# A hybrid decoder step: the samples' attention in pairs and column groups, spread over the third group's attention blocks, and page copies beside the projections

## Chip, cores, metric

One core of a Trainium2 chip. The metric is device microseconds of one launch, the median of several runs; a profiled execution gives the trace. Engines are TensorE (PE, with its weight loads PEld), VectorE (DVE), ScalarE (ACT), GpSimd (POOL) and SyncE (SP), which here issues all DMAs from one queue in order.

## The reference, cut

One layer over a prompt of 2048 tokens and over 8 samples of one token each, D = 1024, f32. The mixer runs two head groups side by side: gated delta rule (4 heads) and sparse attention (4 heads, 2 key heads, 128 wide), then an output projection and a SwiGLU feed-forward of width 2816. For the samples the sparse attention reads a paged cache of 1024 past keys (8 pages of 128 tokens, found through `page_table`):

```python
score = einsum('bqh,bqhs->bqs', iw, relu(einsum('bqhd,bsd->bqhs', iq, ik_all)))  # 8 index heads of 64
_, idx = top_k(score, 256)              # of 1025 keys: 1024 from pages, 1 new
ks, vs = cache_k[phys, off], cache_v[phys, off]      # the new key where idx is the last
s = einsum('bqgrd,bqkgd->bqgrk', q, ks) * 128 ** -0.5
o = einsum('bqgrk,bqkgd->bqgrd', softmax(s), vs)     # 2 key heads g, 2 queries r each
```

The kernel does not gather: it scores all 1025 keys and gives those that aren't selected a large negative bias (L1132 adds it by a product).

## The kernel before

The program is written with tiles in pools; a planner orders each engine's instructions by a simulated timeline. Of the instructions that are ready in its simulation it takes the one that stands first in the program, so later work is pulled ahead wherever inputs and buffers allow. The tags of a pool name sets of buffers in rotation. PSUM has eight banks: "d" x4 (dense products), "g" x2 and "s" x2 (everything else).

Phase 1 (`phase1`): `project(g)` for four groups of 512 tokens, with the samples in group 0; `modulate` for the conditioning; `chunks(g)` for the delta rule; and `first_attn` for attention blocks 0 to 3 (128 tokens each). Phase 2 (`groups`): attention blocks 4 to 15 (`attn`, which calls `index` for scores and selection and `attend` for keys, softmax and values) beside feed-forward blocks `ffn(0)` to `ffn(3)`. `ffn(g)` needs attention of its own four blocks; `ffn(3)` also holds the samples' rows and needs `oTs`, the samples' mixer output. Dense products are three-fold splits (`mm3`, L157 to L159); weights come through `weights` (load at L140 or, kept, L135; split on ACT L141 and DVE L142), three tiles ahead.

In program order of `groups`: attention 4 to 7, 8 to 11, `ffn(0)`, then `copy_pages` (192 page copies, DRAM to DRAM, 64 each of index keys, keys and values, L446 and L447, each after loading the page's number into a register of SP), `sample_gdn` (the samples' delta rule), attention 12 to 15, `ffn(1)`, `sample_steps`, `ffn(2)`, `ffn(3)`.

`sample_steps` goes sample by sample. Index scores: eight transposes of [128 tokens, 64] (L1096), a copy on ACT (L1097), the heads' products with 8 columns (L1100), relu (L1101), and the weighted sum over heads with 8 columns (L1102). Selection: `select`. Keys: per sample one load of 1 MB (L1122), for each key head and half of the pages four transposes into a "g" bank (L1127), a copy on ACT (L1129) and a product with 32 columns (L1130), all accumulating in rows 0 to 31 of two "s" banks. Softmax on 32 rows. Values: one load of 1 MB per sample (L1157), eight products with 32 columns (L1164).

`attend` stores its block at L1380; `ffn` loads those at L1427, splits them at L1428 and L1429, builds rows from the modulation at L1389 and adds gated results at L1419 and L1420.

Of the kernel before, what the change touches and what calls it, by code (L numbers as in the profile page):

```python
# [34 lines left out]
NS = 8  # L35
# [20 lines left out]
WR, WI = 2, 3  # L56

# [4 lines left out]
def const_tables():  # L62
# [18 lines left out]
    s32 = np.zeros((128, 32), np.float32)  # L81
    for kv in range(2):
        for s in range(8):
            for r in range(2):
                s32[s, kv * 16 + s * 2 + r] = 1.0
    parts["s32"] = s32
    d32 = np.zeros((128, 8), np.float32)
    d32[:32] = s32[:8, :].T
    parts["d32"] = d32
    parts["pw"] = np.tile((0.5 ** np.arange(1, SEARCH + 1)).astype(np.float32), (128, 1))  # L90
    parts["io"] = np.tile(np.arange(16, dtype=np.float32), (128, 1))
    off, cols = {}, 0
    for k, v in parts.items():
        off[k] = (cols, v.shape[1])
        cols += v.shape[1]
# [9 lines left out]
CF, COFF, CL = const_tables()  # L105


class K:
# [84 lines left out]
    def build(self):  # L193
        tc, nc = self.tc, self.nc
        with ExitStack() as es:
# [10 lines left out]
            self.ikp_d = self.dr.tile([NS, 128, NPAGE, 64], F32, name="ikp_d")  # L206
# [14 lines left out]
    def consts(self):  # L221
# [4 lines left out]
        cf = self.cf = cp.tile([128, CF.shape[1]], F32, name="cf")  # L226
# [3 lines left out]
        def c(k):  # L230
            o, n = COFF[k]
            return cf[:, o:o + n]
# [7 lines left out]
        self.s32 = c("s32")  # L240
        self.d32 = c("d32")
# [13 lines left out]
        self.iqTs = cp.tile([64, NS, 8], F32, name="iqTs")  # L255
        self.ikTs = cp.tile([128, NS], F32, name="ikTs")
# [10 lines left out]
    def modulation(self):  # L267
# [34 lines left out]
        nc.sync.dma_start(self.cf[:, 128:], A["cf"][:, 128:])  # L302
# [81 lines left out]
    def phase1(self, es):  # L384
# [49 lines left out]
    def copy_pages(self):  # L434

        nc, A, tc = self.nc, self.A, self.tc
        pt_i = self.p2.tile([1, NS * NPAGE], mybir.dt.int32, name="pt_i")
        nc.sync.dma_start(pt_i, A["page_table"].rearrange("n g -> (n g)").unsqueeze(0))
        n_phys = A["cache_k"].shape[1]
        for dst, src in ((self.ikp_d, A["cache_idx_k"][0]), (self.kp_d, A["cache_k"][0].rearrange("g t h d -> g t (h d)")),  # L440
                         (self.vp_d, A["cache_v"][0].rearrange("g t h d -> g t (h d)"))):
            for s in range(NS):
                for g in range(NPAGE):
                    with tc.manual_schedule(engines={nc.sync.engine}):
                        i = s * NPAGE + g
                        pg = nc.sync.value_load(pt_i[0:1, i:i + 1], min_val=0, max_val=n_phys - 1)  # L446
                        nc.sync.dma_start(dst[s, :, g, :], src[ds(pg, 1)].rearrange("a t c -> (a t) c"))  # L447
# [78 lines left out]
    def narrow(self, g, smT, samp):  # L526
# [59 lines left out]
        for t in range(nb):  # L586
# [6 lines left out]
            if t == 4:  # L593
                nc.sync.dma_start(O[9][0, :, 0, :], ik[:NS, 0, :])
                pk = self.ps.tile([128, 512], F32, name="d", tag="d", bufs=4)
                nc.tensor.transpose(pk[:64, :NS], ik[:NS, 0, :], self.id[:NS, :NS])
                nc.scalar.copy(self.ikTs[:64], pk[:64, :NS])
                continue
# [45 lines left out]
    def tok(self, what, blk, pd, rows):  # L644
# [45 lines left out]
        else:  # L690
            self.rope(a[R].rearrange("p (h d) -> p h d", h=8), self.ri, blk, rows, 8, 8, "ropei")
            if samp:
                for h in range(8):
                    nc.tensor.transpose(pt[:64, h * rows:(h + 1) * rows], a[R, h * 64:(h + 1) * 64], self.id[R, R])
                nc.scalar.copy(self.iqTs.rearrange("p n h -> p h n"), pt[:64, :64].rearrange("p (h n) -> p h n", h=8))
# [251 lines left out]
    def sample_gdn(self):  # L947
        nc, p, A, O = self.nc, self.p2, self.A, self.O
        raws = self.raws
        tl, at = p.tile([128, 832], F32, name="gs", bufs=1), [0]  # L950
# [10 lines left out]
        def big():  # L961
            return p.tile([128, 512], F32, name="gS", tag="gS", bufs=2)
# [85 lines left out]
    def sample_steps(self, general):  # L1048
# [4 lines left out]
        def P():  # L1053
            return self.ps.tile([128, 512], F32, name="g", tag="g", bufs=2)

        def P2():
            return [self.ps.tile([128, 512], F32, name="s", tag="s", bufs=2) for _ in range(2)]

        def big():
            return q.tile([128, T], F32, name="big", tag="big", bufs=2)  # L1060

        def mid():
            return q.tile([128, 512], F32, name="PT", tag="PT", bufs=2)

        b0 = q.tile([128, T + 18], F32, name="sc", tag="sc", bufs=2)
        wk, pr = b0[:NS, 0:NK], b0[:32, NK + 16:2 * NK + 16]
        b = q.tile([128, 512], F32, name="oT", tag="oT", bufs=OB)
        PT = b[:, 0:256].rearrange("p (g r) -> p g r", g=NPAGE)
        b = b[:, 256:]
        iwT, ws, nw, dg, pnT, st = b[:8, 0:8], b[:8, 8:72], b[:8, 72:88], b[:32, 88:96], b[:NS, 96:128], b[:32, 128:131]  # L1070
        qk = b[:, 132:164]

        pw = P()
        nc.tensor.transpose(pw[:8, :8], self.iw[:NS, 16, :], self.id[:NS, :NS])
        nc.vector.tensor_copy(iwT, pw[:8, :8])
        nc.vector.memset(ws, 0.0)
        nc.vector.tensor_copy(ws[:, 0:64:9], iwT)

        pw = P()
        for s in range(NS):  # L1080
            nc.tensor.matmul(pw[:8, s:s + 1], self.iqTs[:, s, :], self.ikTs[:64, s:s + 1], start=True, stop=True)
        nc.scalar.activation(nw[:, 0:8], pw[:8, :8], AF.Relu)
        nc.vector.tensor_tensor(nw[:, 0:8], nw[:, 0:8], iwT, op=OP.mult)
        pw = P()
        nc.tensor.matmul(pw[:NS, 0:1], nw[:, 0:8], self.ones[:8, 0:1], start=True, stop=True)
        nc.vector.tensor_copy(wk[:, PAST:NK], pw[:NS, 0:1])
        psc = P2()
        for s in range(NS):
            ikp = mid().rearrange("p (g c) -> p g c", g=NPAGE)
            nc.sync.dma_start(ikp, self.ikp_d[s])  # L1090
            b = big()
            ikT, rl = b[:64, 0:1024], b[:8, 1024:2048]
            for a in range(2):
                pt = P()
                for g in range(4):
                    nc.tensor.transpose(pt[:64, g * 128:(g + 1) * 128], ikp[:, a * 4 + g, :], self.id)  # L1096
                nc.scalar.copy(ikT[:, a * 512:(a + 1) * 512], pt[:64])  # L1097
            for a, (c0, c1) in enumerate(CH):
                pd = P()
                nc.tensor.matmul(pd[:8], self.iqTs[:, s, :], ikT[:, c0:c1], start=True, stop=True)  # L1100
                nc.scalar.activation(rl[:, c0:c1], pd[:8], AF.Relu)  # L1101
                nc.tensor.matmul(psc[a][:NS], ws[:, s * NS:(s + 1) * NS], rl[:, c0:c1], start=s == 0, stop=s == NS - 1)  # L1102
        for a, (c0, c1) in enumerate(CH):
            nc.vector.tensor_copy(wk[:, c0:c1], psc[a][:NS])
# [3 lines left out]
        else:  # L1108
            self.select(q, b0[:NS], q.tile([128, T], BF, name="bias", tag="bias", bufs=2)[:NS, :NK], None, NK, NS, wk)

        qp = q.tile([128, 512], F32, name="qT", tag="qT", bufs=1).rearrange("p (k s r) -> p k s r", k=2, s=NS)
        nc.gpsimd.memset(qp, 0.0)
        for kv in range(2):
            for s in range(NS):
                c = kv * 16 + s * 2
                nc.gpsimd.tensor_copy(qp[:, kv, s, c:c + 2], self.qTs[:, kv * 2:kv * 2 + 2, s])
            nc.vector.tensor_tensor(qk[:, kv * 16:kv * 16 + 16].rearrange("p (n r) -> p r n", r=2), self.qTs[:, kv * 2:kv * 2 + 2, :],
                                    self.kTs[:, kv, :].unsqueeze(1).to_broadcast([128, 2, NS]), op=OP.mult)
        pss = P2()
        for s in range(NS):  # L1120
            kp = big().rearrange("p (g c) -> p g c", g=NPAGE)
            nc.sync.dma_start(kp, self.kp_d[s])  # L1122
            for kv in range(2):
                for a in range(2):
                    pt = P()
                    for g in range(4):
                        nc.tensor.transpose(pt[:, g * 128:(g + 1) * 128], kp[:, a * 4 + g, kv * 128:(kv + 1) * 128], self.id)  # L1127
                    kT = mid()
                    nc.scalar.copy(kT, pt)  # L1129
                    nc.tensor.matmul(pss[a][:32], qp[:, kv, s, :], kT, start=s == 0 and kv == 0, stop=False)  # L1130
        for a, (c0, c1) in enumerate(CH):
            nc.tensor.matmul(pss[a][:32], self.s32[:NS, :], wk[:, c0:c1], start=False, stop=True)  # L1132
            nc.vector.tensor_copy(pr[:, c0:c1], pss[a][:32])
        pw = P()
        nc.tensor.matmul(pw[:32, 0:1], self.s32[:NS, :], wk[:, PAST:NK], start=True, stop=False)
        nc.tensor.matmul(pw[:32, 0:1], qk, self.ones[:, 0:1], start=False, stop=True)
        nc.vector.tensor_copy(pr[:, PAST:NK], pw[:32, 0:1])
# [5 lines left out]
        pp = P()  # L1143
        for g in range(NPAGE):
# [419 lines left out]
```

## Time and profile before

| what | value |
|---|---|
| median of 3 runs | 3913.4 us (3911.79 to 3915.15) |
| the profiled execution | 3911.62 us, span 3909.8 us |
| granted TensorE clock, mean | 0.945 |
| PE busy | 3570.4 us, 91% |
| DVE, ACT, POOL busy | 55%, 39%, 17% |
| DMA | 528.56 MB, mean 135 GB/s |

The span is what the profiler saw from the first to the last instruction; the execution's own time is some 2 us longer. Busy shares are means over stages with different limits, so a change is read from the stage in which it stands: phase 1 up to about 1520 us, attention beside feed-forward up to about 3170 us, and the samples' attention and the last feed-forward block behind it.

### The profile page before, as it was taken

How to read it: one execution, taken by the hardware profiler on the slowest of the kernel's cores; microseconds unless marked ns; L12 is line 12 of the kernel's file. 1: busy time of each engine (PE TensorE's matmuls, PEld its weight loads, DVE VectorE, ACT ScalarE, POOL GpSimd, SP SyncE). 2: the span in 40 equal slices, each digit the busy share in tenths (PEclk: the TensorE clock that was granted, in tenths of full speed). 3: DMA queues.
4: the chain of work that ended last, by engine and by line, in shares of the span. 5: the costliest groups of instructions: out<-in, count | busy, mean ns of one | idle time of the engine just before them, and what ended most of it. 6: DMA issues, size and time to landing. Idle time of an engine off the chain costs nothing.

```text
span 3909.8 us, 60971 instructions
## 1 busy us (share of the span) xinstructions
PE 3570.4 (91%) x22476; PEld 2735.7 (70%) x22476; DVE 2152.3 (55%) x4423; ACT 1513.5 (39%) x2923; POOL 645.4 (17%) x577
## 2 busy tenths in 40 slices
PE   8898888898798789999988999999999999889996
PEld 4766776776586577777766887876777763567774
DVE  3555544562664565866677667676655433244444
ACT  3233223232332433554465545445553334122232
POOL 1001000000000111211131111351111222112213
PEclk9898998898899789999999999999999999999998
DMA  6663454363465334355444333344323334322221
GB/s 238 214 233 124 148 199 129 134 236 128 152 194 197 116 98 143 109 159 163 138 149 130 102 95 105 100 131 161 99 87 105 95 100 175 114 96 84 78 84 66
DMA packets 371767, 528.56 MB, mean 135 GB/s; under 512 B 46020, under 2 KB 250857, under 8 KB 369402
## 3 DMA queue, kind: packets, MB, share of 16 engines
q1 hardware_dynamic: 371458, 524.56, 41.9%
q8 instruction: 179, 2.93, 0.3%
q14 instruction: 130, 1.06, 0.1%
HBM read 427.04 MB, written 116.36 MB: 139 GB/s over the span
## 4 chain that ended last, share of the span: by engine, by line
PE 50%; DVE 8%; DMA 6%; ACT 5%; issue 4%; POOL 2%; SPq 1%; ACTq 0%; DVEq 0%; POOLq 0%
PE d L157 12%; PE d L158 12%; PE d L159 12%; PE s L1303 2%; PE g L1371 2%; DVE wi L142 2%; PE s L1346 2%; DMA wr<-in_w_ffn_in_dram 1%; ACT wi L141 1%; ACT bias L1202 1%; DMA wr<-in_w_ada_dram 1%; PE g L1365 1%; DMA wr<-in_w_ffn_out_dram 1%; PE g L173 1%; PE s L1130 1%
## 5 line engine op out<-in xcount | busy, mean ns | idle before, releaser
L142 DVE TENSOR_TENSOR wi<-wr,wi 128x512 fp32r<-128x512 f32 x712 | 527.9, 746 | 740.5 <-ACT wi L141 729.4
L141 ACT CAST wi<-wr 128x512 fp32r<-128x512 f32 x712 | 437.6, 619 | 940.9 <-PE d L159 372.2
L157 PE MATMUL d<-hh,wi 128*128 128x512 f32 x1792 | 726.7, 406 | 17.1 <-DVE th L1490 12.5
L158 PE MATMUL d<-hl,wi 128*128 128x512 f32 x1792 | 709.3, 396 | 0.0
L159 PE MATMUL d<-hh,wi 128*128 128x512 f32 x1792 | 663.8, 398 | 0.2 <-DVE wi L142 0.2
L1420 POOL TENSOR_TENSOR xt<-xt,tm 128x512 f32<-128x512 f32 x224 | 326.8, 1474 | 547.7 <-DVE tm L1419 506.2
L157 PEld LDWEIGHTS d<-hh,wi 128*128 128x128 f32 x1792 | 339.4, 189 | 104.7 <-DVE th L1490 14.8
L159 PEld LDWEIGHTS d<-hh,wi 128*128 128x128 f32 x1792 | 337.8, 189 | 83.5 <-issue 9.3
L158 PEld LDWEIGHTS d<-hl,wi 128*128 128x128 f32 x1792 | 339.5, 189 | 72.7 <-issue 7.9
L157 PE MATMUL d<-wi,hh 128*128 128x512 f32 x768 | 303.1, 415 | 16.5 <-DMA wi<-kept 10.5
L158 PE MATMUL d<-wi,hh 128*128 128x512 f32 x768 | 309.4, 403 | 0.0
L159 PE MATMUL d<-wi,hl 128*128 128x512 f32 x768 | 306.7, 401 | 0.0
L1496 POOL TENSOR_TENSOR al<-ca,ah 128x512 fp32r<-128x512 f32 x88 | 123.5, 1418 | 1062.6 <-ACT ah L1495 1002.1
L157 PE MATMUL d<-wi,ah 128*128 128x512 f32 x704 | 265.4, 410 | 17.0 <-DVE th L1490 5.6
L158 PE MATMUL d<-wi,ah 128*128 128x512 f32 x704 | 276.8, 396 | 0.5 <-DVE wi L142 0.4
L159 PE MATMUL d<-wi,al 128*128 128x512 f32 x704 | 272.2, 398 | 0.0
L1312 DVE SCALAR_TENSOR_TENSOR sc<-rl,iw,sc 128x512 f32<-128x512 f32 (+3 forms) x224 | 182.5, 815 | 81.0 <-ACT rl L1305 72.2
L1202 ACT ACTIVATE bias<-sc,sv 128x640 bf16<-128x640 f32 (+12 forms) x130 | 181.3, 1394 | 62.7 <-DVE sv L1200 39.6
L1305 ACT ACTIVATE rl<-s 128x512 f32<-128x512 f32 (+3 forms) x288 | 148.0, 543 | 113.3 <-PE s L1303 61.7
L157 PEld LDWEIGHTS d<-wi,hh 128*128 128x128 f32 x768 | 148.7, 195 | 55.9 <-DMA wi<-kept 11.2
L1419 DVE TENSOR_TENSOR tm<-d,row 128x512 f32<-128x512 f32 x224 | 150.6, 683 | 66.4 <-POOL xt L1420 32.7
L1303 PE MATMUL s<-ik,iqT 128*128 128x512 f32 (+3 forms) x576 | 161.1, 388 | 13.3 <-ACT rl L1305 10.6
(510 smaller groups left out, 5569.5 us busy)
## 6 DMA issues: line engine op xcount, KB each, us to landing
wr<-in_w_ffn_in_dram SPq DMA_DIRECT2D x704, 128.0 KB
wi<-kept SPq DMA_DIRECT2D x168, 512.0 KB
wr<-in_w_ffn_out_dram SPq DMA_DIRECT2D x176, 256.0 KB
kept<-wi SPq DMA_DIRECT2D x56, 512.0 KB
xt<-in_x_prompt_dram SPq DMA_DIRECT2D x8, 2048.0 KB
wr<-in_w_ada_dram SPq DMA_DIRECT2D x64, 256.0 KB
wr<-in_w_out_dram SPq DMA_DIRECT2D x64, 256.0 KB
wr<-in_w_in_dram SPq DMA_DIRECT2D x56, 256.0 KB
```

Of the source, the lines that this page charges most:

```text
L141: nc.scalar.copy(w[:, 0], wr)
L142: nc.vector.tensor_tensor(w[:, 1], wr, w[:, 0].bitcast(F32), op=OP.subtract)
L157: nc.tensor.matmul(out, wh, xh, start=start, stop=False, **kw)
L158: nc.tensor.matmul(out, wh, xl, start=False, stop=False, **kw)
L159: nc.tensor.matmul(out, wl, xh, start=False, stop=stop, **kw)
L1202: nc.scalar.activation(c, s, AF.Sign, bias=t, accum_out=cnt)
L1303: nc.tensor.matmul(ps[:, :w], iq[:, h, :].bitcast(F32R), B["ikT"][c * 2 + a][:, :w].bitcast(F32R), start=a == 0, stop=a == 1)
L1305: nc.scalar.activation(r[:, :w], ps[:, :w], AF.Relu)
L1312: nc.vector.scalar_tensor_tensor(s, r[:, :w], iw, s, op0=OP.mult, op1=OP.add)
L1419: nc.vector.tensor_tensor(tm[:rows], pd[:rows], rw, op=OP.mult)
L1420: nc.gpsimd.tensor_tensor(xt, xt, tm[:rows], op=OP.add)
L1496: nc.gpsimd.tensor_tensor(al[b], a, ah[b].bitcast(F32), op=OP.subtract)
```

## The change

`sample_steps` becomes a generator with four parts, and `attn` runs one part ahead of each of blocks 8 to 11:

```diff
-        self.attn(range(8, 12), B, general, 12)
+        self.attn(range(8, 12), B, general, 12, self.sample_steps(general))
         self.ffn(0)
         if not general:
-            self.copy_pages()
             self.sample_gdn()
         self.attn(range(12, 16), B, general)
         self.ffn(1)
-        self.sample_steps(general)
...
         for j, i in enumerate(blocks):
+            if part is not None:
+                next(part)
             if i not in self.biases:
```

Part 1 is the index scores and the selection, part 2 the scores of the first half of the pages, part 3 those of the second half and the softmax, part 4 the values. Index keys of two samples lie side by side in 128 rows (`ikp_d` is [4 pairs, 128, 8 pages, 2, 64]; `iqB` holds the queries of a pair as block-diagonal columns, `ikP` the new index keys), so a transpose and a product serve two samples. Products with 32 columns go to four groups of 32 PSUM rows of one bank in turn: index scores by pair, key scores by key head and sample parity, values by page modulo 4. One product over 128 rows then sums index heads, the softmax runs on 128 rows, and a product with `f4` (four stacked unit matrices) sums the four value groups:

```diff
+        for a, (c0, c1) in enumerate(CH):
+            kT = [keys(self.ikp_d[n, :, a * 4:a * 4 + 4].rearrange("p g e c -> p g (e c)")) for n in range(4)]
+            ps = P("s")
+            for n in range(4):
+                nc.tensor.matmul(ps[n * 32:n * 32 + 32], self.iqB[:, n, :], kT[n], start=True, stop=True)
+            nc.scalar.activation(rl[:, c0:c1], ps, AF.Relu)
+            pw = P()
+            nc.tensor.matmul(pw[:NS], ws, rl[:, c0:c1], start=True, stop=True)
...
+            ps = P("s")
+            nc.tensor.matmul(ps, self.s128[:NS, :], wk[:, c0:c1], start=True, stop=False, skip_group_check=True)
+            for n in range(4):
+                kT = [keys(self.kp_d[n * 2 + j % 2, :, a * 4:a * 4 + 4, j // 2 * 128:j // 2 * 128 + 128]) for j in range(4)]
+                for j in range(4):
+                    nc.tensor.matmul(ps[j * 32:j * 32 + 32], qp[:, j // 2, n * 2 + j % 2, :], kT[j], start=False, stop=n == 3, skip_group_check=True)
+            nc.scalar.copy(pr[:, c0:c1], ps)
...
+            for g2 in range(4):
+                vp = s2().rearrange("p (g c) -> p g c", g=2)
+                nc.sync.dma_start(vp, self.vp_d[s, :, g2 * 2:g2 * 2 + 2])
+                for b in range(2):
+                    g = g2 * 2 + b
+                    j = slice(g % 4 * 32, g % 4 * 32 + 32)
+                    nc.tensor.matmul(po[j, :256], z[:, g, :], vp[:, b, :], start=s == 0 and g < 4, stop=False, skip_group_check=True)
```

`keys` is new: it loads a key tile (256 KB), makes four transposes into a "g" bank and copies them on ACT. Its tiles come from a new tag "s2" of eight 2 KB buffers, longer rows from "s4" (two); `sample_gdn` draws on the same two tags, and the attention's own buffers are no longer used by the samples:

```diff
+        def keys(src):
+            kp, kT, pt = s2().rearrange("p (g c) -> p g c", g=4), s2(), P()
+            nc.sync.dma_start(kp, src)
+            for g in range(4):
+                nc.tensor.transpose(pt[:, g * 128:(g + 1) * 128], kp[:, g, :], self.id)
+            nc.scalar.copy(kT, pt)
+            return kT
```

`copy_pages(which)` moves into phase 1; the page table's tile moves from the second phase's pool to the first's:

```diff
                 self.modulate(g + 2)
                 if g == self.ng - 2:
                     self.modulate(5)
+                self.copy_pages(g)
```

`which` 0, 1 and 2 are index keys, keys and values. In `project(0)` the samples' index queries and keys are written twice, into `iqB` and `ikP`. The rotary tables (1224 columns) move to the first phase's pool and are freed after it; constants `s128`, `d128` and `f4` replace `s32` and `d32`.

More of the change, by code (lines that the diff above doesn't have):

```diff
@@ L92, in const_tables @@
     off, cols = {}, 0
+    for k in ("ra", "ri"):
+        parts[k] = parts.pop(k)
     for k, v in parts.items():
@@ L431, in phase1, with copy_pages @@
                     self.modulate(5)
+                self.copy_pages(g)
         self.ends()
-    def copy_pages(self):
+    def copy_pages(self, which):
         nc, A, tc = self.nc, self.A, self.tc
-        pt_i = self.p2.tile([1, NS * NPAGE], mybir.dt.int32, name="pt_i")
-        nc.sync.dma_start(pt_i, A["page_table"].rearrange("n g -> (n g)").unsqueeze(0))
+        if which == 0:
+            self.pt_i = self.p1.tile([1, NS * NPAGE], mybir.dt.int32, name="pt_i")
+            nc.sync.dma_start(self.pt_i, A["page_table"].rearrange("n g -> (n g)").unsqueeze(0))
+        pt_i = self.pt_i
         n_phys = A["cache_k"].shape[1]
[L440 to L447, printed above, removed]
+        dst, src = ((self.ikp_d, A["cache_idx_k"][0]), (self.kp_d, A["cache_k"][0].rearrange("g t h d -> g t (h d)")),
+                    (self.vp_d, A["cache_v"][0].rearrange("g t h d -> g t (h d)")))[which]
+        for s in range(NS):
+            for g in range(NPAGE):
+                with tc.manual_schedule(engines={nc.sync.engine}):
+                    i = s * NPAGE + g
+                    pg = nc.sync.value_load(pt_i[0:1, i:i + 1], min_val=0, max_val=n_phys - 1)
+                    to = dst[s // 2, :, g, s % 2, :] if which == 0 else dst[s, :, g, :]
+                    nc.sync.dma_start(to, src[ds(pg, 1)].rearrange("a t c -> (a t) c"))
     def load_x(self, g):
@@ L595, in narrow @@
                 pk = self.ps.tile([128, 512], F32, name="d", tag="d", bufs=4)
-                nc.tensor.transpose(pk[:64, :NS], ik[:NS, 0, :], self.id[:NS, :NS])
-                nc.scalar.copy(self.ikTs[:64], pk[:64, :NS])
+                nc.vector.tensor_copy(ik[:NS, 1, :], ik[:NS, 0, :])
+                nc.tensor.transpose(pk[:, :NS], ik[:NS].rearrange("p a c -> p (a c)"), self.id[:NS, :NS])
+                for e in range(2):
+                    nc.scalar.copy(self.ikP[e * 64:e * 64 + 64], pk[e * 64:e * 64 + 64, e:NS:2])
                 continue
@@ L692, in tok @@
             if samp:
-                for h in range(8):
-                    nc.tensor.transpose(pt[:64, h * rows:(h + 1) * rows], a[R, h * 64:(h + 1) * 64], self.id[R, R])
-                nc.scalar.copy(self.iqTs.rearrange("p n h -> p h n"), pt[:64, :64].rearrange("p (h n) -> p h n", h=8))
+                for b in range(2):
+                    x = self.m("iqs")[:NS, :512].rearrange("p (h a c) -> p h a c", h=4, a=2)
+                    for e in range(2):
+                        nc.scalar.copy(x[:, :, e, :], a[R, b * 256:(b + 1) * 256].rearrange("p (h c) -> p h c", h=4))
+                    for h in range(4):
+                        nc.tensor.transpose(pt[:, (b * 4 + h) * NS:(b * 4 + h + 1) * NS], x[:, h].rearrange("p a c -> p (a c)"), self.id[R, R])
+                for e in range(2):
+                    E = slice(e * 64, e * 64 + 64)
+                    nc.scalar.copy(self.iqB[E, :, e * 8:e * 8 + 8], pt[E, :64].rearrange("p (h n a) -> p n a h", h=8, a=2)[:, :, e, :])
                 return
@@ L1051, in sample_steps @@
         CH = ((0, 512), (512, 1024))
[L1053 to L1065, printed above, removed]
@@ L1076, in sample_steps, with P, s2 @@
-        nc.vector.memset(ws, 0.0)
-        nc.vector.tensor_copy(ws[:, 0:64:9], iwT)
-        pw = P()
[L1080 to L1083, printed above, removed]
+        def P(tag="g"):
+            return self.ps.tile([128, 512], F32, name=tag, tag=tag, bufs=2)
+        def s2():
+            return q.tile([128, 512], F32, name="s2", tag="s2", bufs=S2)
@@ L1084, in sample_steps @@
         pw = P()
-        nc.tensor.matmul(pw[:NS, 0:1], nw[:, 0:8], self.ones[:8, 0:1], start=True, stop=True)
+        nc.tensor.matmul(pw[:NS, 0:1], ws, rl[:, PAST:NK], start=True, stop=True)
         nc.vector.tensor_copy(wk[:, PAST:NK], pw[:NS, 0:1])
[L1087 to L1102, printed above, removed]
@@ L1108, in sample_steps @@
         else:
-            self.select(q, b0[:NS], q.tile([128, T], BF, name="bias", tag="bias", bufs=2)[:NS, :NK], None, NK, NS, wk)
-        qp = q.tile([128, 512], F32, name="qT", tag="qT", bufs=1).rearrange("p (k s r) -> p k s r", k=2, s=NS)
+            self.select(q, w0, s4(2 * S4, BF)[:NS, :NK], None, NK, NS, wk, "s")
+        yield
+        qp = s2()
         nc.gpsimd.memset(qp, 0.0)
+        nc.gpsimd.memset(qk, 0.0)
         for kv in range(2):
[L1114 to L1130, printed above, removed]
@@ L1153, in sample_steps @@
+        PZ = s2().rearrange("p (x g c) -> p x g c", x=2, g=NPAGE)
         nc.gpsimd.memset(PZ, 0.0)
-        po = P2()[0]
+        po = P("s")
         for s in range(NS):
-            vp, z = big().rearrange("p (g c) -> p g c", g=NPAGE), PZ[:, s % 2]
-            nc.sync.dma_start(vp, self.vp_d[s])
-            rows = lambda w, n: w[:, :, n * 2:n * 2 + 2], lambda w, n: w[:, :, 16 + n * 2:18 + n * 2]
-            for row in rows:
+            z = PZ[:, s % 2]
+            for kv in range(2):
+                c = lambda n: slice((kv * 2 + n % 2) * 8 + n // 2 * 2, (kv * 2 + n % 2) * 8 + n // 2 * 2 + 2)
@@ L1160, in sample_steps @@
                 if s >= 2:
-                    nc.gpsimd.memset(row(z, s - 2), 0.0)
-                nc.gpsimd.tensor_copy(row(z, s), row(PT, s))
-            for g in range(NPAGE):
-                nc.tensor.matmul(po[:32, :256], z[:, g, :], vp[:, g, :], start=s == 0 and g == 0, stop=False)
-        nc.tensor.matmul(po[:32, :256], pnT, self.vs[:NS, :], start=False, stop=True)
-        o = mid()[:32, :256]
-        nc.scalar.copy(o, po[:32, :256])
+                    nc.gpsimd.memset(z[:, :, c(s - 2)], 0.0)
@@ L1278, in first_attn, with attn @@
         self.attn((i0, i0 + 1), B, False)
-    def attn(self, blocks, B, general, then=None):
+    def attn(self, blocks, B, general, then=None, part=None):
         for j, i in enumerate(blocks):
+            if part is not None:
+                next(part)
             if i not in self.biases:
```

122 lines of the change are left out of this document (77 added, 45 removed).

## The prediction

> **What bounds the kernel now.** I read the page's busy times first, then busy time by stretches, then the groups of instructions, then the order of time on PE and on the DMA queue.
>
> ```profile
> span 3909.8 us, 60971 instructions
> PE 3570.4 (91%) x22476; PEld 2735.7 (70%) x22476; DVE 2152.3 (55%) x4423; ACT 1513.5 (39%) x2923; POOL 645.4 (17%) x577
> ```
> ```profile
> 0.00:400.00 400.00, 348.57 (x2439) 260.91 (x2440) 195.76 (x445) 127.84 (x286) 25.87 (x40) 0.90 0.59 201
> 1540.00:1920.00 380.00, 357.96 (x1569) 281.38 (x1569) 262.98 (x556) 194.02 (x375) 73.06 (x52) 0.99 0.50 145
> 1920.00:2130.00 210.00, 187.02 (x811) 141.55 (x811) 155.82 (x309) 120.44 (x224) 54.85 (x42) 0.96 0.43 137
> 2130.00:2600.00 470.00, 465.48 (x2131) 373.42 (x2130) 325.81 (x637) 230.57 (x377) 106.86 (x73) 1.00 0.34 103
> ```
> Columns of the second fence: stretch, length, then PE, PEld, DVE, ACT, POOL busy with counts, granted clock, DMA share, GB/s. PE bounds: from 2130 to 2600 us, where attention of one group lies beside the feed-forward block of another, it is idle for 4.5 of 470 us. An instruction added to PE there lengthens the run by its full duration; one taken out of a place where PE works alone shortens it as fully.
>
> The samples' attention is such a place. The next rows are PE's first product line of the dense layers (L157) in stretches late in the run (PE busy, PEld busy, clock, DMA).
>
> ```profile
> 3262.50:3311.60 49.10, 0.00 (x0) 0.00 (x0) 0.93 0.49 171
> 3311.60:3328.30 16.70, 0.00 (x0) 0.00 (x0) 0.88 0.34 126
> 3328.30:3368.70 40.40, 0.19 (x1) 0.26 (x2) 0.92 0.44 156
> ```
> For 106.2 us (3262.5 to 3368.7) no dense product runs: the samples' keys (49.1), softmax (16.7) and values (40.4) are alone, and the last feed-forward block waits for their result.
>
> ```profile
> L1127 PE MATMUL g<-cf,big 128*128 128x128 f32 x128 | 22.1, 300 | 0.2 <-DMA big<-kp_d 0.2
> L1130 PE MATMUL s<-PT,qT 128*32 128x512 f32 x64 | 34.7, 625 | 0.0
> L1164 PE MATMUL s<-big,iqT 128*32 128x256 f32 x128 | 31.7, 407 | 5.2 <-DMA big<-vp_d 4.2 <-POOL iqT L1162 0.9
> L1102 PE MATMUL s<-big,oT 8*8 8x512 f32 x32 | 17.4, 629 | 0.1
> L1100 PE MATMUL g<-big,iqTs 64*8 64x512 f32 x32 | 17.0, 619 | 0.0
> L1096 PE MATMUL g<-cf,PT 128*64 128x128 f32 x64 | 10.5, 289 | 0.0
> ```
> Busy us stand after the bar. Each f32 product is two instructions (L1130: 64 for 32 products), a transpose is one.
>
> **Part 1: what leaves the end of the run.** The lone 106.2 us go. The index scores (L1096, L1100, L1102) take 10.5 + 17.0 + 17.4 = 44.9 us of PE; 4.2 of them are in the lone stretch already:
>
> ```profile
> 3262.96 1.88 PE L1100 MATMUL g<-big,iqTs 64*8 64x512 f32 x4
> 3264.77 2.29 PE L1102 MATMUL s<-big,oT 8*8 8x512 f32 x4
> ```
> The other 40.7 were taken from feed-forward block 2, except for about 8 (my estimate) that filled PE's hole while block 2 hands over to block 3: that hole is late next, with no sample work to cover it. So 40.7 - 8 = 33, and 139 us leave the end.
>
> **Part 2: what is added beside the third group's attention.** Transposes: 32 for index keys (two samples share one, 64 before), 128 for keys, 8 for probabilities: 168 x 22.1/128 = 0.173, 29 us. Products 512 wide: 8 for index scores (16), 2 for the weighted sum over heads (16), 32 for keys, 2 for the mask: 44. Values: 64 products 256 wide. Their price among dense products:
>
> ```profile
> 3180.50 0.40 PE L157 MATMUL d<-hh,wi 128*128 128x512 f32 x1
> 3180.73 0.40 PE L158 MATMUL d<-hl,wi 128*128 128x512 f32 x1
> 3181.06 1.02 PE L1100 MATMUL g<-big,iqTs 64*8 64x512 f32 x2
> 3182.01 0.50 PE L159 MATMUL d<-hh,wi 128*128 128x512 f32 x1
> 3182.35 0.40 PE L157 MATMUL d<-hh,wi 128*128 128x512 f32 x1
> 3357.07 7.25 PE L1164 MATMUL s<-big,iqT 128*32 128x256 f32 x32 [1.40 <-DMA big<-vp_d]
> ```
> From start to start one wide product holds PE 0.95 us (3181.06 to 3182.01), and the steps into it and after it are 0.33 and 0.34 where dense products follow each other by 0.23 (3180.50 to 3180.73): a visit to the narrow shape costs 0.2 more. A value product costs 7.25/16 = 0.45. One by one: 29 + 44 x 0.95 + 64 x 0.45 = 100, with some 60 visits 112 us. The change writes four products into four column groups of one bank. Whether four run together the trace shows for 32x32 tiles only:
>
> ```profile
> L747 PE MATMUL g<-Dm,E 32*32 32x32 f32 x2048 | 31.8, 200 | 9.2 <-DVE Dm L742 6.5 <-issue 2.4
> L765 PE MATMUL g<-Dm,NT 32*32 32x32 f32 x256 | 13.5, 226 | 0.2 <-issue 0.2
> ```
> L747 walks four array positions and takes 15.5 ns an instruction; L765 stays in one for eight products at a time and takes 52.7: a factor of 3.4. If all packed by four, it would be 29 + (10 + 4) x 0.95 + 16 x 0.45 + 28 visits x 0.2 = 55. I take 90, nearer the upper end: a key tile becomes ready alone, after its four transposes and a 0.586 us copy on ACT (row below), so the planner will put dense work between products of one set; only the values, two pages per load, come in pairs.
>
> The Trainium skill, "TensorEngine Tiling (Array Packing)", section Key Properties, says that changing the tiling mode drains the engine; the 0.33 and 0.34 us steps agree. Its section PSUM Bottleneck says that packing speeds the products and not the evacuation, which speaks against this change, and I weigh it as a rival. "TensorE: Matmul & The Clock Gate", section Measured speedup vs the span model, gives 2.38 for three column tiles; as an estimate that would make 71 us of products 30, and the sum 31 us lower than mine; no run here shows it yet.
>
> **Part 3: what hides or uncovers.** PE idles 210 - 187 = 23 us between 1920 and 2130; sample work may fill 0 to 16, I take 8. Loads: 72 smaller ones (256 KB) replace 24. PE works in order, so a late one now stops dense work too. Bounds: 0, and 32 value loads x 1.4 us (the wait on L1164 above) = 45; I take 5, as eight buffers run ahead where there were two. The doubled index key and extra copies in the projection touch 8 rows: between 0 and 4 us, I take 1. Constants moved between pools: no added work on a path, 0.
>
> **Part 4: page copies.**
>
> ```profile
> L447 SPq DMA_DIRECT2D ikp_d<-in_cache_idx_k_dram x64: 493/502/632, 1543.7 to 1673.3; - x64
> L447 SPq DMA_DIRECT2D vp_d<-in_cache_v_dram x64: 493/500/539, 1802.2 to 1919.3; - x64
> 1546.89 3.06 SPq L447 DMA_DIRECT2D ikp_d<-in_cache_idx_k_dram  x3
> L966 SPq DMA_DIRECT2D out_dram<-in_state_conv_dram x1: 823/823/823, 35.7 to 35.7; - x1
> ACT wi L141 <- DMA wr<-in_w_ffn_in_dram: 60.1, 28, 6.0
> ACT wi L141 <- DMA wr<-in_w_ffn_in_dram: 27.8, 18, 5.2
> ```
> The last two rows are waits in 1540 to 1920 and in 2130 to 2600. The 192 copies hold SP (3.06 us for three, about 1.28 from start to start) from 1543 to 1919 with weight loads queued behind them; PE idles 22 us there against 3.6 (4.5 x 380/470) in as long a stretch without copies. So leaving gains 0 to 18. Where they go, PE idles 51.4 of the first 400 us and DMA is at 0.59. L966, also a copy from DRAM to DRAM, stands far down the program and is issued at 35.7 us: a copy that needs nothing is pulled ahead. The page copies then need only the page table and can land in the first projection. Bounds there: a loss of 0 to 36 (twice 18, as the share starts at 0.59 rather than 0.34). I take -8 and +8, net 0.
>
> **Part 5: the attention's own pace.** Sample tiles take PSUM slots "s" and "g", two each, from the blocks beside them, and a score bank is held through 16 key tiles.
>
> ```profile
> 2474.95 0.43 SPq L1380 DMA_DIRECT2D oT_d<-oT  x1
> L1015 PE MATMUL g<-gs,gS x64: 165/250/353, 2522.3 to 2603.7; 128*128 128x1 f32 x64
> 2597.81 1.56 SPq L1427 DMA_DIRECT2D ca<-oT_d  x2
> 3167.48 0.38 SPq L1380 DMA_DIRECT2D oT_d<-oT  x1
> 3171.35 0.17 PE L1074 MATMUL g<-cf,iw 8*8 8x8 f32 x1
> 3213.46 1.74 SPq L1427 DMA_DIRECT2D ca<-oT_d  x2
> 3234.35 0.40 PE L159 MATMUL d<-wi,al 128*128 128x512 f32 x1
> 3365.89 0.24 PE L1170 MATMUL g<-cf,PT 32*128 32x32 f32 x1 [0.28 <-DVE oTs L1171]
> L1129 ACT COPY PT<-g x32: 558/586/587, 3268.5 to 3318.0; 128x512 f32<-128x512 f32 x32
> ```
> L1380 stores blocks 11 and 15; L1427 are the first loads of feed-forward blocks 2 and 3: slack of 123 and 46 us. L1074 and L1170 begin and end the sample's stage, the L159 row is block 2's last dense product, L1015 the sample's delta-rule part. A key tile took 49.5/31 = 1.6 us alone; 40 tiles are 64 us, softmax about 8 (half of the 16.7 us stretch), values (no "g") half of 40: a delay D of 92. Block 2's dense work ends at 3235 in the trace, tail included about 3236; less 33, plus 90 - 8 + 5, it ends at 3290, and block 15 must be stored some 20 us earlier: D matters above 3290 - 20 - 3167 = 103. Bounds: 0, and 97 if D is the some 200 us that the sample's stage lasts (3171 to 3366, and its first loads). D is close to 103, so I take 10.
>
> **Sum**: -139 + 90 - 8 + 5 + 1 + 0 + 10 = -41. The profiled execution took 3911.6 us (span 3909.8), within 0.05% of the median 3913.4. Forecast: 3870.
>
> **Rivals.** (a) The groups pack by four and the holes fill: -139 + 55 - 16 + 2 + 1 = -97, 3815. For: L747. Against: tiles ready one by one. (b) Nothing packs, as the ACT copy paces every key tile: 112 in place of 90, loads 10, otherwise the same: -14, 3898. For: the 32 copies stay as they were. (c) The other side: attention becomes the end of block 2. Every "g" slot that the sample holds delays the blocks in full; with D = 200 it is -51 + 97 = +46, 3958. It is slower than before once D passes 103 + 51 + 8 = 162. For: the delta-rule part (L1015) ran at 2522 to 2604, behind block 11 and ahead of block 12, so such work does not slip between attention blocks. Against: index scores and selection use no "g" and can go on meanwhile. (d) The copies do not go to the later projections but to the start, where they cost 36 and leaving gains nothing: -41 + 36, 3907.
>
> **How the numbers follow.** A measurement of this kernel can't tell less than about 0.2%, 8 us, from no change. Chances: forecast 0.44 (its own range 3845 to 3895), (a) 0.14, (b) 0.16, (c) 0.18, (d) 0.08. Faster: 0.44 + 0.14, most of (b) and a little of (d), 0.71; same: the rest of (b), half of (d), a little of (c), 0.09; slower 0.20. The range 3815 to 3930 leaves out half of (a) and two thirds of (c), 0.19.
>
> **What would show it.** Right: no stretch without L157 around 3260 to 3370, its end 40 us earlier, the sample's products between about 1950 and 2600 with PE at 97% or more, and block 15 stored before block 2's last product. Part 2 is wrong if the sample's PE groups sum to below 60 or above 115 us; part 4 if PE's idle in the first 400 us grows by over 15; part 5 if PE is idle between block 15's attention and the last feed-forward block. I would be wrong altogether if DMA waits appear on PE at the key products.

## The result, and the profile after

The changed kernel is slower: 3952.7 us (median of 4, 3950.4 to 3964.0) against 3912.7 for the kernel before in the same measurement, a ratio (of the means) of 1.0107 with a 95% interval of [1.0087, 1.0127]. The forecast was 3870 within 3815 to 3930: wrong in sign, and 23 us outside the range.

The head of the page after, and busy time in the stretches that the prediction showed of before (length, then PE, PEld, DVE, ACT, POOL with counts, granted clock, DMA share, GB/s):

```profile
span 3952.8 us, 60820 instructions
PE 3568.1 (90%) x22394; PEld 2746.4 (69%) x22394; DVE 2134.7 (54%) x4424; ACT 1501.8 (38%) x2909; POOL 650.0 (16%) x571
```
```profile
0.00:400.00 400.00, 315.91 (x2185) 228.59 (x2185) 157.77 (x366) 108.21 (x249) 20.98 (x38) 0.88 0.67 222
1540.00:1920.00 380.00, 369.85 (x1672) 297.34 (x1673) 272.70 (x566) 190.36 (x368) 73.95 (x60) 1.00 0.38 116
1920.00:2130.00 210.00, 194.46 (x809) 141.15 (x807) 133.87 (x283) 115.68 (x218) 63.90 (x54) 0.95 0.38 121
2130.00:2600.00 470.00, 468.03 (x2068) 346.56 (x2069) 248.01 (x462) 205.20 (x344) 80.82 (x77) 0.99 0.39 120
```
PE's busy time is the same as before (3570.4), so the loss is idle time: 32.7 us more of it in the first 400 us (84.1 after, 51.4 before). From 1540 to 1920, which the copies have left, idle fell from 22 to 10.

Stores and loads on SP that mark the stages, before and then after (L932 and L951 store the delta rule, L1380 and L1407 an attention block, L1454 loads feed-forward input):

```profile
1522.30 0.38 SPq L932 DMA_DIRECT2D oT_d<-dec  x1
1962.59 0.38 SPq L1380 DMA_DIRECT2D oT_d<-oT  x1
```
```profile
1574.85 0.38 SPq L951 DMA_DIRECT2D oT_d<-dec  x1
1979.68 0.38 SPq L1407 DMA_DIRECT2D oT_d<-oT  x1
2651.55 0.33 SPq L1454 DMA_DIRECT2D ca<-oT_d  x1
2747.62 0.36 SPq L1407 DMA_DIRECT2D oT_d<-oT  x1
2749.97 0.34 SPq L1454 DMA_DIRECT2D ca<-oT_d  x1
3327.15 1.56 SPq L1454 DMA_DIRECT2D ca<-oT_d  x2
3411.91 0.36 SPq L1407 DMA_DIRECT2D oT_d<-oT  x1
3414.20 0.81 SPq L1454 DMA_DIRECT2D ca<-oT_d  x2
```
With the rows that the prediction shows of before, the span divides so:

| stage | before | after | change |
|---|---|---|---|
| to the last delta-rule store of phase 1 | 1522.3 | 1574.9 | +53 |
| to the first load of feed-forward block 2 | 1075.5 | 1076.7 | +1 |
| to the first load of block 3 | 615.7 | 675.6 | +60 |
| to the end | 696.3 | 625.7 | -71 |

The last stage gained half of what Part 1 had promised, as feed-forward block 3 now waits for attention block 15; phase 1 and the stage of block 2 lost more. Attention block 7 is stored only 17 us late, though phase 1 ended 53 late: without copies attention 4 to 7 made up 36. Then blocks 8 to 11 took 768 us (2747.62 - 1979.68) where they took 512. Feed-forward block 2 waits for block 11, and block 3 for block 15; the first dense product line in two stretches after (PE busy, PEld busy, clock, DMA):

```profile
2700.00:2750.00 50.00, 0.00 (x0) 0.00 (x0) 0.76 0.30 102
3370.00:3412.00 42.00, 0.00 (x0) 0.00 (x0) 0.88 0.14 42
```
In both no such product runs, and the loads of the attention heads' rows (2749.97, 3414.20) follow the stores of blocks 11 and 15 by 2.3 us. From feed-forward block 3's first dense product on, the two kernels do the same, before (from 3368.5) and after (from 3412.9):

```profile
3368.50:3909.80 541.30, 484.85 (x2111) 368.46 (x2110) 239.06 (x344) 156.16 (x294) 134.37 (x112) 0.96 0.26 83
3412.90:3952.80 539.90, 485.26 (x2111) 369.23 (x2110) 239.32 (x344) 158.55 (x298) 140.63 (x116) 0.95 0.28 85
```
So the whole loss stands in the start of that block: 44 us later, 1 us after the store of block 15, which came 244 us later than before (3411.91 against 3167.48): 17 up to block 7, 256 in blocks 8 to 11, less 28 in blocks 12 to 15 (664 us for 693).

### The profile page after: what moved, and what is told of

The parts are those of the page before. It is cut to its first block, busy times and chain, and to the rows that moved or that the text cites. A ratio compares the mean times of both kernels' runs of the same rounds, so it can differ in the third digit from the quotient of the medians.

```text
span 3952.8 us, 60820 instructions
## 1 busy us (share of the span) xinstructions
PE 3568.1 (90%) x22394; PEld 2746.4 (69%) x22394; DVE 2134.7 (54%) x4424; ACT 1501.8 (38%) x2909; POOL 650.0 (16%) x571
## 4 chain that ended last, share of the span: by engine, by line
PE 56%; DVE 7%; DMA 4%; issue 3%; ACT 3%; POOL 1%; SPq 0%; ACTq 0%; DVEq 0%; POOLq 0%
PE d L160 13%; PE d L161 13%; PE d L162 13%; PE g L1398 3%; PE s L1330 2%; PE s L1373 2%; PE g L1392 1%; DVE wi L145 1%; DMA wr<-in_w_ada_dram 1%; PE g L176 1%; PE s L1148 1%; PE g L177 1%; ACT wi L144 1%; DMA ca<-oT_d 1%; DMA wi<-kept 1%
## 5 line engine op out<-in xcount | busy, mean ns | idle before, releaser
L160 PE MATMUL d<-hh,wi 128*128 128x512 f32 x1792 | 726.2, 406 | 13.9 <-ACT wi L144 7.2
L160 PEld LDWEIGHTS d<-hh,wi 128*128 128x128 f32 x1792 | 339.3, 189 | 105.0 <-ACT wi L144 10.7
L160 PE MATMUL d<-wi,hh 128*128 128x512 f32 x768 | 304.4, 421 | 48.4 <-ACT wi L144 20.8
L160 PE MATMUL d<-wi,ah 128*128 128x512 f32 x704 | 262.1, 408 | 4.8 <-DVE tm L1446 2.5
L160 PEld LDWEIGHTS d<-wi,hh 128*128 128x128 f32 x768 | 147.6, 194 | 95.4 <-ACT wi L144 25.7
L1229 ACT ACTIVATE bias<-sc,sv 128x640 bf16<-128x640 f32 (+11 forms) x120 | 169.7, 1414 | 56.1 <-DVE sv L1227 32.5
```

The lines of the kernel that those rows point to most:

```text
L160: nc.tensor.matmul(out, wh, xh, start=start, stop=False, **kw)
L1229: nc.scalar.activation(c, s, AF.Sign, bias=t, accum_out=cnt)
```

## Experiments

Theory A: the page copies, where they went, are the loss. Theory B: the parts are, as they delay attention.

**Taking the change apart.** Four kernels. In the first, the copies go back to phase 2, ahead of attention block 4:

```diff
-                self.copy_pages(g)
...
+            for k in range(3):
+                self.copy_pages(k)
         self.attn(range(4, 8), B, general, 8)
```


> The changed kernel with the page copies issued at the start of the second phase (ahead of attention block 4), so that the first phase has none. Theory A (the copies, pulled to 40 to 436 us, cost the first phase 52 us, and their absence gave about 30 back beside feed-forward block 0): the last delta-rule store is back at about 1522 us instead of 1575, block 7 is stored some 20 us earlier than in the changed kernel, and the time is about 3930. Rival (the first phase lost its time to other edits, such as the doubled index queries in the projection): the last delta-rule store stays beyond 1560 and the time beyond 3945.

4114.1, ratio 1.0539 [1.0521, 1.0556]: far off for either theory. The copies did not slip in between other loads but went out in one block, 64 of them first (index keys) and 64 last (values):

```profile
L457 SPq DMA_DIRECT2D ikp_d<-in_cache_idx_k_dram x64: 493/494/613, 1531.4 to 1613.2; - x64
L457 SPq DMA_DIRECT2D vp_d<-in_cache_v_dram x64: 493/494/523, 1697.3 to 1778.9; - x64
```
```profile
1530.00:1780.00 250.00, 0.00 (x0) 0.00 (x0) 0.52 0.26 79
```
The second fence is that kernel's first dense line: nothing for 250 us. 192 copies are 1.29 us of SP each (248/192), and weight and attention loads stand behind them. Before, the same copies lay among weight loads, where they stood behind that work in the program.

Only the copies moved, all else as before:

> The kernel before with the page copies alone moved to the first phase; the samples' attention is the old one in its old place. Theory A: the first phase ends about 52 us later, feed-forward block 0 gains 15 to 32 back, 3930 to 3950. Rival (the copies only move within slack): 3905 to 3920.

3948.5, 1.0107 [1.0090, 1.0124]. In the old kernel the copies alone cost as much as the whole change.

The parts put back behind `ffn(1)`, copies left in phase 1; then both moves undone, so that only the new form is left:

```diff
-        self.attn(range(8, 12), B, general, 12, self.sample_steps(general))
+        self.attn(range(8, 12), B, general, 12)
...
         self.ffn(1)
+        for _ in self.sample_steps(general):
+            pass
```


> The changed kernel with all four parts of the samples' attention run in the old place, behind feed-forward block 1 in the program; the copies stay in the first phase. Theory B (the parts delay the attention blocks, which then hold up feed-forward blocks 2 and 3): blocks 11 and 15 are stored about 1 to 2 us a block from the old distances to block 7 (512 and 1205 us behind it, as before, instead of 768 and 1432), and the time is that of the copies-only kernel less 30 to 50: about 3900. Rival (it is not the place but the new form, its loads and column groups, that cost): 3945 or more.

> The changed kernel with both moves undone: parts in the old place, copies issued where they were before; only the new form of the samples' attention is left. If the new form saves what its PE groups say (index scores about 29 us less, values 17 less, in stretches where PE is alone or the bound): 3865 to 3880. Rival (its key tiles keep the pace of the copies on ACT and nothing else was on the path): 3900 to 3915.

3961.4 (1.0133 [1.0116, 1.0150]) and 3925.5 (1.0044 [1.0027, 1.0061]). The first lies where its rival had it, the second beyond both: the new form in the old place is slower than the old one. Against 3908.3 the new form costs 17, the copies 36 to 40 on top, and spreading the parts gains 9 to 10 (3961.4 to 3952.7, or 1.0133 to 1.0107); the intervals of these two overlap, so that gain is the least sure.

**Why the new form lost in the old place.** PE on the lone key tiles of the last of these kernels (L1094 transposes, L1147 products):

```profile
3320.24 0.66 PE L1094 MATMUL g<-cf,s 128*128 128x128 f32 x4
3321.62 1.04 PE L1147 MATMUL s<-s,s 128*32 128x512 f32 x2 [0.72 <-ACT s L1095]
3322.59 0.66 PE L1094 MATMUL g<-cf,s 128*128 128x128 f32 x4
```
A tile takes 2.35 us, 0.72 of it idle for the copy on ACT; before, it took 1.6. Each tile holds two of eight small buffers, one for its load and one for its copy. The next kernel loads the keys of two samples for four pages into a wide buffer (two DMAs of 512 KB) and leaves the eight to the copies:

```diff
-                kT = [keys(self.kp_d[n * 2 + j % 2, ...]) for j in range(4)]
+                kb = q.tile([128, T], F32, name="big", tag="big", bufs=2)...
+                for e in range(2):
+                    nc.sync.dma_start(kb[:, e], self.kp_d[n * 2 + e, :, a * 4:a * 4 + 4, :])
+                kT = [keys(None, kb[:, j % 2, ...]) for j in range(4)]
```


> The new form in the old place with the copies in the old place (3925.5 in an earlier run), with one edit: the keys come as 512 KB loads with 4 KB runs into two wide buffers instead of 256 KB loads with 512 B runs into the ring of eight small ones. Theory 'loads': a lone key tile, 2.35 us from start to start with 0.72 of it idle, falls to 1.6 or less, and the time to 3885 to 3905. Theory 'copy' (the ACT copy between transposes and product paces a tile): the tile stays at 2.2 or more and the time at 3915 to 3930.

3889.5, 0.9961 [0.9947, 0.9975]: 36 less by the medians, 32 by the ratios. The idle piece is gone and some products now run in pairs (x4 is two of them), two per 1.05 us:

```profile
3285.85 0.66 PE L1096 MATMUL g<-cf,big 128*128 128x128 f32 x4
3286.44 1.05 PE L1152 MATMUL s<-s,s 128*32 128x512 f32 x4
3287.42 0.66 PE L1096 MATMUL g<-cf,big 128*128 128x128 f32 x4
```
Larger loads and freed buffers came together; which of them did it isn't separated. The Trainium skill, "DMA: Bandwidth & Descriptors", section Rules for kernel authors, advises to coalesce many small transfers, and says that under 64 KB one pays mostly overhead; the direction agrees here, though these loads had 256 KB and PE's wait in the small form was put down to key loads for only 10.0 us. The largest wait left in this kernel:

```profile
PE s L1145 <- DVE s L1249: 16.9, 1, 16.9
```
L1145 is the mask's product, which opens each score bank in the new form, so no key product runs until the selection (L1249) is done. In the old form it closed the bank.

```diff
-            nc.tensor.matmul(ps, self.s128[:NS, :], wk[:, c0:c1], start=True, stop=False, skip_group_check=True)
...
-                    nc.tensor.matmul(ps[j * 32:j * 32 + 32], ..., start=False, stop=n == 3, skip_group_check=True)
+                    nc.tensor.matmul(ps[j * 32:j * 32 + 32], ..., start=n == 0, stop=False, skip_group_check=True)
+            nc.tensor.matmul(ps, self.s128[:NS, :], wk[:, c0:c1], start=False, stop=True, skip_group_check=True)
```


> The form that took 3889.5 us (new form in the old place, copies in the old place, keys in wide loads) with one edit: the selection mask is added to the key scores as the last product of a bank instead of the first, as the old form has it. There PE waits 16.9 us in one piece at the mask's product for the selection, with no dense work left to cover it. Theory 'mask gates the keys': the key tiles run during the selection, and the time falls by 10 to 20, to 3870 to 3880. Rival: the two score banks hold the wait, which only moves to the first bank's end: 3884 to 3892.

3867.5, 0.9880 [0.9857, 0.9902]: 22 less by the medians, 32 by the ratios, more than the 10 to 20 expected.

**Why the copies cost.** First the same copies from another queue (`nc.gpsimd` for `nc.sync`):

> The changed kernel with one edit: the 192 page copies of the projections are issued on POOL's DMA queue instead of SP's. Theory 'queue' (the copies cost because each holds SP for about 1.28 us and weight loads stand behind them): the last delta-rule store comes back from 1575 to about 1525 us and the time falls by 36 to 40, to about 3915. Theory 'traffic' (the copied bytes take the DMA engines from the weight loads, whichever queue issues them): the store stays at 1565 to 1580 and the time at 3945 to 3960.

3964.3, 1.0152 [1.0135, 1.0169]; phase 1 ended at 1565. Inconclusive: the block of copies moved to POOL, and what POOL owes the delta rule stood behind it (who waited for whom, 190 to 320 us).

```profile
DVE rnz L853 <- POOL rnz L193: 56.6, 1, 56.6
```
Then the same bytes in 24 issues; the lookup in the page table, and with it the load of each page's number into a register, is left out:

```diff
         for s in range(NS):
-            for g in range(NPAGE):
-                ...
-                    nc.sync.dma_start(to, src[ds(pg, 1)].rearrange("a t c -> (a t) c"))
+            to = dst[s // 2, :, :, s % 2, :] if which == 0 else dst[s]
+            nc.sync.dma_start(to, src[s * NPAGE:(s + 1) * NPAGE].rearrange("g t c -> t g c"))
```


> The changed kernel with the page copies of the first phase made in 24 large transfers instead of 192: the same bytes, an eighth of the issues. It leaves out the lookup in the page table (pages in order). Theory 'queue' (192 issues of about 1.28 us hold the weight loads up): last delta-rule store from 1575 to 1525 to 1540, time 3910 to 3925. Theory 'traffic' (the bytes hold them up): the store at 1565 or later, PE's idle in the first 500 us at 110 us or more (after: 113), time 3945 to 3965.

3925.2, 1.0040 [1.0028, 1.0052], 27 below the changed kernel. The first 500 us of before, of after and of this kernel:

```profile
0.00:500.00 500.00, 438.04 (x3678) 336.06 (x3679) 253.44 (x597) 154.00 (x363) 28.87 (x46) 0.90 0.57 192
```
```profile
0.00:500.00 500.00, 386.87 (x3315) 287.75 (x3316) 219.03 (x532) 138.12 (x320) 28.58 (x45) 0.86 0.62 204
```
```profile
0.00:500.00 500.00, 403.71 (x3485) 306.25 (x3486) 229.95 (x557) 147.37 (x352) 26.66 (x46) 0.88 0.64 215
```
PE's idle is 62, 113 and 96 us, and phase 1 ends at 1522, 1575 and 1552: neither theory alone. The 168 issues fewer, with their register loads, give back 23 of phase 1's 53 us; 29 stay, with the same bytes, which here came in one burst. (The profiled execution of this kernel took 3911.9, 13 less than its median, so the 23 may be somewhat high.) "DMA: Bandwidth & Descriptors" of the Trainium skill, section Issuing engines are not separate DMA queues, says that another issuing engine only saves the time to initiate, usually small beside the transfer; here 168 issues fewer gave back 23 of 53 us.

**Where else the copies could stand.** Between attention 4 to 7 and 8 to 11, the parts as in the change:

> The changed kernel with one edit: the page copies stand in the second phase again, between the attention of blocks 4 to 7 and of blocks 8 to 11. If the copies in the first phase are the whole loss: 3905 to 3920, the spread parts then being worth nothing or little. If the delay of attention is a loss of its own that the copies hid: first phase back at about 1522, block 11 still about 250 us late against block 7, and 3925 to 3960.

4008.2, 1.0266 [1.0248, 1.0283], worse than either case: again one block, 1535 to 1811 us.

**Why attention is late.** The held score bank taken away (each set of four key products in its own bank, which DVE adds up):

> The changed kernel with one edit: each set of four key products goes to a PSUM bank of its own, which VectorE adds up in SBUF, so no score bank is held through 16 key tiles. Theory 'held bank' (attention crawls because the sample keeps one of two score banks): blocks 9 and 10, which now take 204 and 220 us, take 150 or less, block 15 is stored 80 us or more earlier, the waits ahead of feed-forward blocks 2 and 3 go, and the time is 3895 to 3915. Theory 'turns' (the sample's tiles take turns with attention for the other slots and for PE, held bank or not): blocks 9 and 10 stay near 200 and the time at 3940 to 3960.

3985.5, 1.0206 [1.0189, 1.0223]; blocks 9 and 10 took 257 and 263 us, where they took 204 and 220 in the change. Giving the bank back did not help, though the edit brings sums on DVE and more "s" tiles of its own. The sample's transposes in the four banks of the dense layers (tag "d" for "g" in `keys`):

> The changed kernel with one edit: the sample's index keys and keys are transposed into the four PSUM banks of the dense layers instead of the two that attention's own transposes and sums use. Theory 'slots' (the sample's tiles take attention's PSUM slots): blocks 9 and 10 fall from 204 and 220 us to 160 or less each, block 15 is stored 80 us or more earlier, 3900 to 3930. Theory 'order' (the sample's work stands ahead of attention in the order in which PE and ACT are filled, whatever the banks): blocks 9 and 10 at 185 or more, 3940 to 3965.

4118.0, 1.0524 [1.0500, 1.0549]. Blocks 8, 9 and 10 now took 81, 74 and 133 us (1756.5 to 2044.7). That does not show that the banks held attention back, because up to 1923 us attention had no dense work beside it; with that work back, block 11 took 224 (to 2269.0), where it took 170 in the change. What the run shows is that the wait went to the dense layers. Their first product line, then PE where the sample's last key tiles end:

```profile
1500.00:1900.00 400.00, 0.00 (x0) 0.00 (x0) 0.81 0.26 80
```
```profile
1921.54 0.60 PE L1096 MATMUL d<-cf,s 128*128 128x128 f32 x4
1922.77 0.48 PE L160 MATMUL d<-wi,hh 128*128 128x512 f32 x1
1925.46 1.05 PE L1149 MATMUL s<-s,s 128*32 128x512 f32 x2
```
No L160 product for the whole stretch, then the first one 1.2 us after the sample's last transposes, though those kept PE only 27 us of it. A feed-forward block that stands behind the sample in the program gets no bank until the sample has had its last. So in this run the banks went out in program order, and what shared a tag with the sample's tiles waited for all of them. That attention's wait for "g" and "s" in the change is of the same kind is likely, but not shown.

The four parts behind the attention of block 11, all else as in the change:

> The changed kernel with one edit: the four parts stand behind the attention of blocks 8 to 11 in the program instead of among them (ahead of feed-forward block 0 in order). Theory 'order': blocks 8 to 11 go at their old pace (block 11 some 500 us after block 7, where it is 768), and the sample's work fills in behind them, ahead of block 12, which is then late by 100 to 200: 3920 to 3950. Theory 'slots': the sample still takes its turns among blocks 8 to 11 and block 11 stays over 650 us behind block 7; 3945 to 3970.

3965.2, 1.0144 [1.0122, 1.0166]. Blocks 8 to 11 take their old 512 us (1989.8 to 2501.5), and block 12 is stored 589 us later, where before it took 227 (2475.0 to 2702.1):

```profile
2501.45 0.38 SPq L1409 DMA_DIRECT2D oT_d<-oT  x1
3090.05 0.38 SPq L1409 DMA_DIRECT2D oT_d<-oT  x1
```
The sample's products stand between them, from 2506.9 to 2839.9 us, and block 12 is 362 us late: attention that stands behind the sample waits for it here too, and moving the parts moves the delay. What makes the sample long? In the change, key loads were issued some 7 us apart between weight loads, so all key tiles were taken from one load:

> The changed kernel with all 32 key tiles taken from one loaded block: it leaves out 31 of the 32 key loads, and so reads the same keys throughout. All transposes, copies and products stay. Theory 'loads' (the sample's key loads, issued 6 to 7.5 us apart between weight loads, pace its tiles, and attention behind it waits for the tiles): blocks 9 and 10 fall from 204 and 220 us to 160 or less each, block 15 is stored 60 us or more earlier, 3895 to 3925. Theory 'turns' (each transpose, copy and product waits its turn among dense work on PE and ACT): blocks 9 and 10 at 190 or more, 3940 to 3960.

3924.6, 1.0045 [1.0029, 1.0060]. Between the two: 24 to 28 us gained, at the edge of what loads foretold, and block 15 stored 30 earlier, but blocks 9 and 10 took 173 and 187 us and blocks 8 to 11 still 742. The 32 products without a load to wait for were spread over 227 us, 7.1 us a tile; in the change it is 324 us (2156.1 to 2479.9), 10.1 a tile:

```profile
L1152 PE MATMUL s<-s,s x64: 592/605/617, 2158.1 to 2385.5; 128*32 128x512 f32 x64
```
The loads are a part, not the whole. PE itself was never idle meanwhile, in this kernel and then in the change:

```profile
2158.00:2385.00 227.00, 227.00 (x994) 162.92 (x992) 111.94 (x205) 102.06 (x174) 33.84 (x25) 1.00 0.27 84
2160.00:2480.00 320.00, 320.00 (x1374) 232.21 (x1372) 157.91 (x289) 140.96 (x235) 52.24 (x39) 1.00 0.36 109
```
So whatever a tile waited for, PE did other work. That a tile's three steps each wait their turn among that work on PE and ACT is what is left; no run showed it by itself.

**The best form.** New form, old places, wide keys, mask last, and wide loads for the values of every second sample:

> The form with the mask last (3867.5 us) with one edit: the values of every second sample come as one 1 MB load into a wide buffer, which is free by then, so that more of them are under way while the softmax runs. There PE waits 10.2 us for value loads. If the loads can start in the softmax: 5 to 10 us less, 3858 to 3863. If the DMA engines are full in that stretch anyway (share 0.87 from 3300 to 3320): no change, 3864 to 3870.

3856.6, 0.9866 [0.9847, 0.9884]: faster than the kernel before and the change, though its interval overlaps that of the form without wide values. PE's wait for values fell from 10.2 to 5.3:

```profile
PE s L1200 <- DMA s<-vp_d: 5.3, 2, 3.5
```

## Why the prediction was wrong

Part 1 (139 leave the end): the lone stretch went as said, but block 3's first loads (3327.15) came 85 us ahead of the store of block 15 (3411.91), so the last stage gave 71.

Part 2 (90 added): right, and right in its reason. The sample's groups after, then two of attention's; before, those two (L1303, L1371) took 161.1 and 132.9:

```profile
L1148 PE MATMUL s<-s,s 128*32 128x512 f32 x64 | 33.5, 605 | 0.0
L1095 PE MATMUL g<-cf,s 128*128 128x128 f32 x160 | 24.3, 274 | 1.5 <-DMA s<-ikp_d 1.5
L1190 PE MATMUL s<-s,s 128*32 128x256 f32 x128 | 14.7, 390 | 0.0
L1114 PE MATMUL s<-s,iqB 128*32 128x512 f32 x16 | 8.4, 604 | 0.0
L1330 PE MATMUL s<-ik,iqT 128*128 128x512 f32 (+3 forms) x576 | 168.2, 391 | 11.3 <-ACT rl L1332 8.8 <-DMA kT<-kT_d 1.5 <-DVE st L1374 0.4
L1398 PE MATMUL g<-PT,V 128*128 128x256 f32 x504 | 142.0, 404 | 20.9 <-ACT PT L1395 20.8
```
With small groups the sample took some 90 us. Key products came alone (33.5 of 34.7 left), values packed. What was not priced: attention's own products took 7 and 9 us more. The value products (L1398) were as fast beside the sample's key tiles as before (378 ns each from 2160 to 2600, clock 1.00; 385 before from 1970 to 2475), and slow where attention ran alone at a lower granted clock: 528 ns from 2700 to 2750 (0.76) and 450 from 3370 to 3412 (0.88).

Part 3 (5 for loads): too small. Taking away the key loads was worth 24 to 28 us in the spread place, and wide ones, with the buffers that they freed, 32 to 36 in the old place. The sign named for it did not show: PE never waited for a load at the key products (0.0 above), because it did other work meanwhile and the delay fell on attention. The mask's new position, at least 22 us in the old place, was in the diff and not seen.

Part 4 (copies, net 0): the step that failed first. "A copy that needs nothing is pulled ahead" was right, and the place (39.8 to 436.2 us) too; the price was not. The loss taken was 8 of a bound of 36; the copies alone cost 40 in the old kernel, and idle in the first 400 us grew by 33, where over 15 was to show the step wrong. Weights' waits in 0 to 500 us rose from the first row (before) to the second (after):

```profile
ACT wi L141 <- DMA wr<-in_w_in_dram: 53.6, 25, 4.7
```
```profile
ACT wi L144 <- DMA wr<-in_w_in_dram: 123.2, 36, 14.4
```
The whole move cost 36 to 40 net in the old place of the parts, so rival (d)'s price was right, on top of the rest. In the changed kernel its share isn't separated: 17 of the 244 us by which block 15 is late stand before block 8, and fewer issues brought the whole time down by 27. The sign of a sum that stood at -41 with two such terms unsure was less safe than 0.71.

Part 5 (attention's delay D = 92, priced at 10): the second step that failed. D was 256 in blocks 8 to 11, and block 15 was 244 late, against a threshold of 103. D was worked out from a key tile that took 1.6 us alone; among dense work a tile took 10.1, and 7.1 without loads. One reading in it was wrong: the index scores do use "g", as `keys` transposes into it. The threshold was wrong as well. It let block 3 begin 47 us after block 15 is stored (3368.5 - 51 = 3317.5 against 3167.5 + 103 = 3270.5), and it began 1 us after. By its rule 244 us late would have been -51 + 141 = +90, where the start of block 3, and with it the end, moved by 44.

Rival (c), with D = 200 and 3958, named the mechanism and came within 6 us of the result, but by luck: a delay taken too short met a price taken too high, and it had no copies in it. What the change would cost without the copies is not measured. If the pieces add, it is some +8 (17 less 9 or 10), but the two kernels that kept the parts spread and put the copies into phase 2 met a block of copies there.

## What to carry to other kernels

Price a chain that is moved beside a full engine by its steps there, not by its time alone, and ask which later tiles share its PSUM tags: they may wait for its last tile, as the dense layers did here. Many small register-addressed copies were cheap only where they stood behind other loads in the program; ahead of them they were a block of their full issue time. A full engine is no sign of a good place: PE was busy without a gap beside the sample's tiles, and the run still ended later, because the work that the end waited for came late. A smaller product count is worth nothing until loads, buffers and the first product of a bank let the products run; repaired in the old place, the same form gained 1.3%.

## What the runs showed of the hardware

Four column groups do run together. Eight value products take 1.00 us from their start to the next instruction's, 0.45 each one by one before, a factor of 3.6:

```profile
2586.43 1.07 PE L1190 MATMUL s<-s,s 128*32 128x256 f32 x16
2587.43 0.50 PE L1330 MATMUL s<-ik,iqT 128*128 128x512 f32 x1
```
The Trainium skill, "TensorE: Matmul & The Clock Gate", section Measured speedup vs the span model, has 2.38 for three column tiles; this is four, and the same kind of gain.
